# One Strassen product for the v of all attention heads, in place of four plain ones, and a new order of scores and transposes

## The chip, the cores and the metric

The kernel runs on one core of one Trainium2 chip, as one launch. The metric is the device time of the launch in microseconds (us). TensorE, VectorE, ScalarE and GpSimd are named PE, DVE, ACT and POOL in the profile's rows; PEld is TensorE's load of a stationary operand, SP the queue that issues most DMAs.

## The reference

A trunk of two layers on x of 512 tokens by 1024 features, in float32. Each layer is a SwiGLU FFN (hidden width 2816), a mixer, and a second FFN; after each of the six steps stands a layer norm over `alpha * x + step`. The mixer of layer 0 is block-sparse attention with a relative-position bias, that of layer 1 a pooling mixer. With 512 tokens in blocks of 256 the block selection always takes the one past block, so the attention is plain causal attention:

```
qkv = (h @ w_in).reshape(B, S, 3, H, dh)      # w_in 1024 x 3072, H = 8 heads of dh = 128
p   = softmax(q @ k.T * dh**-0.5 + bias[head, distance]), causal
out = concat_heads(p @ v) @ w_out
```

So v of all heads together is one product of h (512 x 1024) with 1024 columns of w_in.

## The kernel before

**Arithmetic.** Every float32 product is made of three matmuls on a high and a low part (`mm3`, lines 105 to 107: high with low, high with high, low with high). `split` (lines 100 and 101) forms the parts: ACT copies the high part, DVE subtracts it from the source for the low one. A weight tile of 128 x 1024 (512 KB) is loaded raw by SP, split into a pair, and called a unit. The FFNs already use Strassen's algorithm in Winograd's form, seven products for eight: a class `Seven` keeps an activation as the operands of the seven products, some of them sums made by `sums` on DVE (`form`, line 314), and a `Quad` holds the weights of one such product in five raw tiles, two of them summed as they are loaded by a GpSimd DMA with accumulation (line 208), and two more sums made on DVE (line 143). A `Plain` activation has only its high and low parts.

**Attention** (`attention`, from line 711) takes the heads in four pairs. For a pair it forms q and k of both heads, feature major (`a_block`: 24 matmuls with 512 tokens moving; in the first pair the tokens come in two halves of 256, since the layer norm before is still being finished), then v of the pair, token major (`values`, line 721: 96 matmuls in two groups of 48, the stationary operand 128 tokens of x, 256 weight columns moving). `scores(h)` is 12 matmuls and a softmax on DVE and ACT (lines 752 to 756). `transposes(h)` turns the probabilities through TensorE (10 transposes, line 764) and splits them; `outputs(h)` is 12 matmuls with v. The order in a pair is: scores of head h, first half of v, scores of head h+1, second half of v, transposes of h; transposes of h+1 and the outputs of both stand among the q and k of the next pair. After the four pairs comes the product with w_out (`BProduct`: `early` for the first four of its eight weight rows, 24 matmuls for each of four token tiles, and `tail`).

**What sets the order.** TensorE's order is that of the program. The instructions of DVE, ACT, POOL and the DMA queues are ordered by the compiler's list scheduler, each engine's queue then runs in order; `tc.issue_after` keeps the instructions of a block behind a given one on its engine. Weight units are split ahead of their use by `run_ahead`, up to `PARTS` = 5 beyond those that were given back by `retire`; raw tiles are loaded ahead by `load_ahead`, at most 9 not yet used up while no slots are held, 6 while `held[0]` is 4, as it is in attention. All of it shares 20 slots of 4 KB per partition. A second pool, `act`, of 9 tiles of 8 KB holds activations; two split weight units stand there as guests (named w) when attention begins. The layer norm's result is staged in `stage` (one tile of 16 KB).

**PSUM.** The eight banks are assigned by hand: in pairs 1 to 3, q and k in 0 and 1, v in 0 and 1, scores in 2, 3 and 4 (4, 5 and 6 for head 0), transposes in 5, 6 and 7, outputs in 2 and 3.

Of the kernel before, what the change touches and what calls it, by code (L numbers as in the profile page):

```python
# [32 lines left out]
P = 128  # L33
S = 512
D = 1024
# [48 lines left out]
def trunk(ctx, tc, x_in, xt, rel_bias, ln_g, ln_b, w_gu, w_dq, w_down, a_in, a_out, b_in, b_group, b_scale, b_out, onehot, out):  # L84
# [80 lines left out]

    def ffn_units(l, m):
# [3 lines left out]
        for i, jj in ORDER:  # L170
# [4 lines left out]
            else:  # L175
                if i == 1:
                    both = [Quad(w_dq[l, m, 2 * (jj - FF) + q]) for q in range(2)]
                    pieces[-10:] = [q.pieces[k] for k in range(5) for q in both]
# [5 lines left out]
    for hp in range(H // 2):  # L184
        for part in (0, 1, 2):
            a_plain(a_in[0], part * D + hp * 256)
    b_plain(a_out[0], range(NK))
# [49 lines left out]
    def run_ahead():  # L237
        load_ahead()
        while len(parts) < min(len(units), retired[0] + PARTS + max(0, free() - 2) // 2 + early[0] + sum(i >= retired[0] for i in guests)):
            prepare()  # L240
            load_ahead()
# [29 lines left out]
    class Plain:  # L271
# [14 lines left out]
        def put(self, t, half, src):  # L286
            hi, lo = self.parts_of(half)
            split(hi[:, :, t * P:(t + 1) * P], lo[:, :, t * P:(t + 1) * P], src)
# [5 lines left out]
    class Seven(Plain):  # L294
# [30 lines left out]
        def seven(self, b11, b21, b12, b22, room):  # L325
# [18 lines left out]
            yield  # L344

# [84 lines left out]
    def halves(x, accs, blocks):  # L430

        for i in range(8):
            a_block(x, accs[i % 4], *blocks[i % 4], 0, 256, range(4 * (i // 4), 4 * (i // 4) + 4))
            if i in LATE:
                late.pop(0)()
                if i == LATE[1]:
                    run_ahead()
# [17 lines left out]
    class BProduct:  # L455
# [35 lines left out]
        def tail(self):  # L491
# [5 lines left out]
            run_ahead()  # L497
# [213 lines left out]
    def attention(n, x, dest):  # L711
        held[0] = 4
        with tc.tile_pool(name="att", bufs=1) as ap:
# [7 lines left out]
            def values(hp, vp, tt):  # L721
                acc = bank(tt, f"v{hp}_{tt}")
                for i in range(2):
                    t = 2 * tt + i
                    for k in range(NK):
                        hi, lo = vp[k // 4]
                        c = slice((k % 4) * 256, (k % 4) * 256 + 256)
                        mm3(acc[:, i * 256:(i + 1) * 256], *x.at(k, t * P, (t + 1) * P), hi[:, c], lo[:, c], k == 0, k == NK - 1)
                if tt == 0:
                    v[hp] = [ap.tile([P, NT, 256], F32R, tag=f"v{i}", name=f"v{i}_{hp}") for i in range(2)]  # L730
                split(v[hp][0][:, 2 * tt:2 * tt + 2, :], v[hp][1][:, 2 * tt:2 * tt + 2, :],
                      acc.rearrange("p (t c) -> p t c", c=256))

            def scores(h):
# [4 lines left out]
                b0 = 2 if h else 4  # L739
# [36 lines left out]
            def outputs(h, b):  # L776
                o = bank(b, f"o{h}")
                vh, vl = v[h // 2]
# [211 lines left out]
```

## Time and profile before

| | |
|---|---|
| time, median of 3 runs | 1702.57 us (1699.46 to 1703.05) |
| profiled execution, its time | 1703.53 us |
| its span, first to last instruction | 1701.8 us |
| TensorE matmuls busy | 1681.0 us (99%) |
| TensorE weight loads busy | 1563.6 us (92%) |
| VectorE busy | 1328.7 us (78%) |
| ScalarE busy | 854.1 us (50%) |
| GpSimd busy | 125.8 us (7%) |
| DMA, mean | 164 GB/s |

A matmul's own duration in the trace is longer than the distance to the next one, since matmuls are pipelined: what one costs is read from the distance between starts, that is, from the length of a stretch with a known count. Attention's pairs stand from 346 to 519 us in the span, its product with w_out behind them.

### The profile page before, as it was taken

How to read it: one execution, taken by the hardware profiler on the slowest of the kernel's cores; microseconds unless marked ns; L12 is line 12 of the kernel's file. 1: busy time of each engine (PE TensorE's matmuls, PEld its weight loads, DVE VectorE, ACT ScalarE, POOL GpSimd, SP SyncE). 2: the span in 40 equal slices, each digit the busy share in tenths (PEclk: the TensorE clock that was granted, in tenths of full speed). 3: DMA queues.
4: the chain of work that ended last, by engine and by line, in shares of the span. 5: the costliest groups of instructions: out<-in, count | busy, mean ns of one | idle time of the engine just before them, and what ended most of it. 6: DMA issues, size and time to landing. Idle time of an engine off the chain costs nothing. (4 is left out here: it accounts for less than half of the span.)

```text
span 1701.8 us, 28140 instructions
## 1 busy us (share of the span) xinstructions
PE 1681.0 (99%) x11451; PEld 1563.6 (92%) x11451; DVE 1328.7 (78%) x1756; ACT 854.1 (50%) x1187; POOL 125.8 (7%) x168
## 2 busy tenths in 40 slices
PE   9999999999999999999999999999999999999997
PEld 9999899898888999989989999799898899998986
DVE  7686988775666878788788787897887887879696
ACT  5454555463444555545555555455454555545460
POOL 1102000000000001100000011000000101111000
PEclk9999999999999999999999999999999999999999
DMA  9779756512345267786683677756624647867541
GB/s 311 190 209 254 199 143 179 178 57 72 109 119 179 51 181 201 191 216 153 160 235 76 176 199 190 214 151 151 221 75 111 174 124 182 215 161 210 150 136 74
DMA packets 91058, 279.87 MB, mean 164 GB/s; under 512 B 8816, under 2 KB 26264, under 8 KB 90928
## 3 DMA queue, kind: packets, MB, share of 16 engines
q1 hardware_dynamic: 71088, 206.07, 36.2%
q0 software_dynamic: 19840, 71.99, 23.6%
q8 instruction: 90, 1.47, 0.4%
q14 instruction: 40, 0.33, 0.1%
HBM read 275.91 MB, written 4.74 MB: 165 GB/s over the span
## 5 line engine op out<-in xcount | busy, mean ns | idle before, releaser
L100 ACT ACTIVATE hi<-raw 128x1024 fp32r<-128x1024 f32 (+1 forms) x469 | 490.0, 1054 | 417.6 <-DVE lo L101 139.6
L101 DVE TENSOR_TENSOR lo<-raw,hi 128x1024 fp32r<-128x1024 f32 (+1 forms) x469 | 568.1, 1218 | 147.8 <-ACT hi L100 138.2
L105 PE MATMUL gu<-x,hi 128*128 128x256 f32 x2344 | 664.1, 283 | 1.2 <-DVE cb L570 0.8
L107 PE MATMUL gu<-x,lo 128*128 128x256 f32 x2344 | 663.6, 283 | 0.8 <-DVE lo L101 0.8
L106 PE MATMUL gu<-x,hi 128*128 128x256 f32 x2344 | 663.4, 283 | 0.0
L105 PEld LDWEIGHTS gu<-x,hi 128*128 128x128 f32 x2344 | 450.0, 192 | 3.7 <-DVE cb L570 1.7
L107 PEld LDWEIGHTS gu<-x,lo 128*128 128x128 f32 x2344 | 449.9, 192 | 1.4 <-DVE lo L101 1.4
L106 PEld LDWEIGHTS gu<-x,hi 128*128 128x128 f32 x2344 | 450.1, 192 | 0.4
L107 PE MATMUL d<-hi,xh 128*128 128x512 f32 x448 | 175.1, 391 | 7.4 <-DVE xh L101 7.4
L105 PE MATMUL d<-lo,xh 128*128 128x512 f32 x448 | 174.8, 390 | 0.2
L106 PE MATMUL d<-hi,xh 128*128 128x512 f32 x448 | 174.5, 389 | 0.0
L143 DVE TENSOR_TENSOR raw<-raw,raw 128x1024 f32<-128x1024 f32 x112 | 136.9, 1222 | 36.9 <-DMA raw<-in_ffn_w_dq 35.0
L208 POOL DMA_DIRECT2D raw<-in_ffn_w_gu x80 | 69.4, 868 | 801.1 <-DMA raw<-in_ffn_w_gu 404.5
L107 PEld LDWEIGHTS d<-hi,xh 128*128 128x128 f32 x448 | 84.1, 188 | 27.4 <-DVE xh L101 10.0
L105 PEld LDWEIGHTS d<-lo,xh 128*128 128x128 f32 x448 | 84.1, 188 | 17.9 <-DVE ca L570 0.6
L106 PEld LDWEIGHTS d<-hi,xh 128*128 128x128 f32 x448 | 84.1, 188 | 17.1
L567 ACT ACTIVATE kept<-gu 128x512 f32<-128x512 f32 x120 | 70.4, 586 | 48.7 <-PE gu L107 48.7
L105 PE MATMUL acc<-lo,h 128*128 128x512 f32 x192 | 75.2, 392 | 0.0
L107 PE MATMUL acc<-hi,h 128*128 128x512 f32 x192 | 74.7, 389 | 0.0
L106 PE MATMUL acc<-hi,h 128*128 128x512 f32 x192 | 74.7, 389 | 0.0
L642 DVE SCALAR_TENSOR_TENSOR ax<-d,ax 128x512 f32<-128x512 f32 x112 | 72.5, 683 | 0.0
L101 DVE TENSOR_TENSOR x<-st,x 128x512 fp32r<-128x512 f32 (+1 forms) x61 | 51.3, 854 | 20.2 <-ACT x L100 19.8
(169 smaller groups left out, 2301.5 us busy)
## 6 DMA issues: line engine op xcount, KB each, us to landing
raw<-in_ffn_w_gu SPq DMA_DIRECT2D x215, 512.0 KB, 4.9
raw<-in_ffn_w_gu POOLq DMA_DIRECT2D x80, 512.0 KB, 6.9
raw<-in_ffn_w_dq SPq DMA_DIRECT2D x80, 512.0 KB, 4.3
raw<-in_ffn_w_dq POOLq DMA_DIRECT2D x32, 512.0 KB, 8.3
raw<-in_ffn_w_down SPq DMA_DIRECT2D x24, 512.0 KB, 4.2
raw<-in_a_w_in SPq DMA_DIRECT2D x24, 512.0 KB, 4.7
ax<-in_ln_b POOLq DMA_DIRECT2D x20, 512.0 KB, 8.1
raw<-in_a_w_out SPq DMA_DIRECT2D x8, 512.0 KB, 5.3
```

The source lines that it names most:

```text
L100: nc.scalar.activation(hi, src, AF.Copy)
L101: return nc.vector.tensor_tensor(lo, src, hi.bitcast(F32), op=ALU.subtract)
L105: nc.tensor.matmul(acc, sh, ml, start=first, stop=False, skip_group_check=shared)
L106: nc.tensor.matmul(acc, sh, mh, start=False, stop=False, skip_group_check=shared)
L107: nc.tensor.matmul(acc, sl, mh, start=False, stop=last, skip_group_check=shared)
L143: nc.vector.tensor_tensor(d, d, more, op=ALU.add)
L208: queued["acc"] = nc.gpsimd.dma_start(p.tile, p.plus, accum_op=ALU.add)
L567: nc.scalar.activation(kept[i, jj], acc, AF.Copy)
L642: nc.vector.scalar_tensor_tensor(r, acc[t], 0.5 / ALPHA * sign, r, op0=ALU.mult, op1=ALU.add)
```

## The change

v of all eight heads is formed at once behind q and k of the first pair, by seven Strassen products. Each has two weight units (halves of the contraction), 24 matmuls with 128 tokens stationary and 512 weight columns moving, and accumulates in two banks. The attention's input becomes `Mixed`: the plain parts, which serve q and k and three of the products, and four summed operands. The weights come from a new input that holds the v columns of w_in rearranged into two quads. Partial results are kept in SBUF (`keep`) and added to later ones on DVE (`added`); `value` splits the sums into v. Scores of heads 0 and 1 and the transposes of head 0 stand between the seven products. In pairs 1 to 3 the order is: q and k of head h; outputs of h-2, transposes of h-1, scores of h; q and k of h+1; outputs of h-1, transposes of h, scores of h+1. Behind the last pair the token tiles of the product with w_out come in the order 0, 1, 3, 2, with the outputs of head 6 and the transposes of head 7 after the first. In `halves`, which the pooling mixer uses too, the weight units beyond the next two and the sums are placed behind the last split of the input. Signature and input lists are left out here, and so are empty lines.

```diff
@@ -162,6 +162,11 @@
     ORDER += [(i, FF + g) for g in range(1, BLOCK // GROUP) for i in LATER]
+    def two_quads(w, i):
+        both = [Quad(w[i + q]) for q in range(2)]
+        pieces[-10:] = [q.pieces[k] for k in range(5) for q in both]
+        return both
@@ -174,16 +179,20 @@
                 if i == 1:
-                    both = [Quad(w_dq[l, m, 2 * (jj - FF) + q]) for q in range(2)]
-                    pieces[-10:] = [q.pieces[k] for k in range(5) for q in both]
+                    both = two_quads(w_dq[l, m], 2 * (jj - FF))
                 for q in both:
                     q.unit(i)
         b_plain(w_down[l, m], range(BLOCK, NF))
     ffn_units(0, 0)
     for hp in range(H // 2):
-        for part in (0, 1, 2):
+        for part in (0, 1):
             a_plain(a_in[0], part * D + hp * 256)
+        if hp == 0:
+            both = two_quads(w_v, 0)
+            for i in LATER:
+                for q in both:
+                    q.unit(i)
     b_plain(a_out[0], range(NK))
@@ -234,9 +243,9 @@
-    def run_ahead():
+    def run_ahead(most=99):
         load_ahead()
-        while len(parts) < min(len(units), retired[0] + PARTS + max(0, free() - 2) // 2 + early[0] + sum(i >= retired[0] for i in guests)):
+        while len(parts) < min(len(units), taken[0] + most, retired[0] + PARTS + max(0, free() - 2) // 2 + early[0] + sum(i >= retired[0] for i in guests)):
             prepare()
@@ -285,7 +294,7 @@
             hi, lo = self.parts_of(half)
-            split(hi[:, :, t * P:(t + 1) * P], lo[:, :, t * P:(t + 1) * P], src)
+            self.last = split(hi[:, :, t * P:(t + 1) * P], lo[:, :, t * P:(t + 1) * P], src)
@@ -343,6 +352,18 @@
+    class Mixed(Seven):
+        put = Plain.put
+        def stationary(self, i, k, t):
+            if i in (4, 5, 6, 7):
+                o = self.parts[i][:, :, k, t * P:(t + 1) * P]
+                return o[:, 0], o[:, 1]
+            half, h = {1: (0, 0), 2: (1, 0), 3: (1, 1)}[i]
+            return self.at(4 * half + k, (2 * h + t) * P, (2 * h + t + 1) * P)
     def to_feature_major(dest, t, half, xn, n):
@@ -427,14 +448,18 @@
-    def halves(x, accs, blocks):
+    def halves(x, accs, blocks, sums=lambda: None):
         for i in range(8):
             a_block(x, accs[i % 4], *blocks[i % 4], 0, 256, range(4 * (i // 4), 4 * (i // 4) + 4))
             if i in LATE:
                 late.pop(0)()
                 if i == LATE[1]:
-                    run_ahead()
+                    while len(parts) < taken[0] + 2:
+                        prepare()
+                    with tc.issue_after(x.last.ins):
+                        run_ahead()
+                        sums()
         for acc, blk in zip(accs, blocks):
@@ -494,7 +519,7 @@
             early[0] = self.guests
-            run_ahead()
+            run_ahead(6)
             for t in range(NT):
@@ -718,25 +743,61 @@
-            def values(hp, vp, tt):
-                acc = bank(tt, f"v{hp}_{tt}")
-                for i in range(2):
-                    t = 2 * tt + i
-                    for k in range(NK):
-                        hi, lo = vp[k // 4]
-                        c = slice((k % 4) * 256, (k % 4) * 256 + 256)
-                        mm3(acc[:, i * 256:(i + 1) * 256], *x.at(k, t * P, (t + 1) * P), hi[:, c], lo[:, c], k == 0, k == NK - 1)
-                if tt == 0:
-                    v[hp] = [ap.tile([P, NT, 256], F32R, tag=f"v{i}", name=f"v{i}_{hp}") for i in range(2)]
-                split(v[hp][0][:, 2 * tt:2 * tt + 2, :], v[hp][1][:, 2 * tt:2 * tt + 2, :],
-                      acc.rearrange("p (t c) -> p t c", c=256))
+            accs, kept = {}, {}
+            def keep(i, acc):
+                kept[i] = ap.tile([P, 2, 512], F32, tag=f"kept{i % 5}", name=f"vkept{i}")
+                for t in range(2):
+                    nc.scalar.activation(kept[i][:, t], acc[t], AF.Copy)
+            def value(t, d, src, sign):
+                hi, lo = v["hi"][:, t, d * 512:(d + 1) * 512], v["lo", t // 2][:, t % 2, d * 512:(d + 1) * 512]
+                if sign == 1:
+                    split(hi, lo, src)
+                else:
+                    nc.scalar.activation(hi, src, AF.Copy, scale=-1.0)
+                    nc.vector.scalar_tensor_tensor(lo, src, -1.0, hi.bitcast(F32), op0=ALU.mult, op1=ALU.subtract)
+            def added(i, acc):
+                k = kept.pop(i)
+                for t in range(2):
+                    nc.vector.tensor_tensor(k[:, t], k[:, t], acc[t], op=ALU.add)
+                return [k[:, t] for t in range(2)]
+            def v_product(i):
+                if i in (1, 2, 5):
+                    accs[BANKS[i]] = [bank({1: 0, 2: 2, 5: 2}[i] + t, f"v{i}_{t}") for t in range(2)]
+                acc = accs[BANKS[i]]
+                for q in range(2):
+                    wh, wl = weights()
+                    for k in range(2):
+                        c = slice(k * 512, (k + 1) * 512)
+                        for t in range(2):
+                            mm3(acc[t], *x.stationary(i, 2 * q + k, t), wh[:, c], wl[:, c], q == 0 and k == 0 and i in (1, 2, 5),
+                                q == 1 and k == 1 and i in (2, 3, 4), True)
+                if i == 2:
+                    v["hi"] = lnp.tile([P, NT, D], F32R, tag="stage", name="vh")
+                if i in (2, 7):
+                    v["lo", len(v) - 1] = glob.tile([P, 2, D], F32R, tag="act", bufs=ACT, name=f"vl{len(v) - 1}")
+                if i in (1, 6, 5):
+                    keep(i, acc)
+                else:
+                    srcs = acc if i == 4 else added({2: 1, 7: 5, 3: 6}[i], acc)
+                    t0, d, sign = {2: (0, 0, 1), 7: (2, 1, -1), 3: (2, 0, 1), 4: (0, 1, -1)}[i]
+                    for t in range(2):
+                        value(t0 + t, d, srcs[t], sign)
+                with tc.issue_after(x.last.ins):
+                    retire(2)
             def scores(h):
                 (qh, ql), (kh, kl) = qk["q", h], qk["k", h]
                 bt = ap.tile([P, S], F32, tag="bias", bufs=2, name=f"bias{h}")
                 nc.sync.dma_start(bt, bass.AP(tensor=gr.tensor, offset=gr.offset + h * P * GW + P - 1,
                                                 ap=[[GW - 1, P], [1, S]]))
-                b0 = 2 if h else 4
+                b0 = 2 if h > 1 else 4
                 b01 = bank(b0, f"s{h}_01")
@@ -775,10 +836,9 @@
                 o = bank(b, f"o{h}")
-                vh, vl = v[h // 2]
-                vc = slice((h % 2) * P, (h % 2 + 1) * P)
+                vc = slice(h * P, (h + 1) * P)
                 for j, (m0, two) in enumerate(pT[h]):
-                    mm3(o[:, m0:], vh[:, j, vc], vl[:, j, vc], two[0], two[1], j == 0, j == NT - 1)
+                    mm3(o[:, m0:], v["hi"][:, j, vc], v["lo", j // 2][:, j % 2, vc], two[0], two[1], j == 0, j == NT - 1)
                 if h % 2 == 0:
@@ -792,37 +852,41 @@
                 if hp == 0:
-                    accs = [bank(i, f"qk0_{i}") for i in range(4)]
-                    for acc, nm in zip(halves(x, accs, blocks), names):
+                    qk_accs = [bank(i, f"qk0_{i}") for i in range(4)]
+                    for acc, nm in zip(halves(x, qk_accs, blocks, x.sums), names):
                         project(acc, *nm)
+                    with tc.issue_after(x.last.ins):
+                        retire(4)
+                    scores(0)
+                    for i in LATER:
+                        v_product(i)
+                        if i == 2:
+                            scores(1)
+                        if i == 7:
+                            transposes(0)
                 else:
                     for i in range(4):
+                        acc = bank(i + 2 if hp == 1 and i < 2 else i % 2, f"qk{hp}_{i}")
+                        a_block(x, acc, *blocks[i])
+                        project(acc, *names[i])
                         if i == 1:
-                            transposes(h - 1)
-                        if i == 2:
-                            outputs(h - 2, 2)
-                        if i == 3:
-                            ins = outputs(h - 1, 3)
+                            ins = outputs(h - 2, 4 if hp == 1 else 0)
                             if hp > 1:
                                 update_residual(ins, 2)
-                        acc = bank(i % 2, f"qk{hp}_{i}")
-                        a_block(x, acc, *blocks[i])
-                        project(acc, *names[i])
-                retire(4)
-                vp = [weights(), weights()]
-                scores(h)
-                values(hp, vp, 0)
-                scores(h + 1)
-                values(hp, vp, 1)
-                retire(2)
-                transposes(h)
+                            transposes(h - 1)
+                            scores(h)
+                        if i == 3:
+                            retire(4)
+                            outputs(h - 1, 0)
+                            transposes(h)
+                            scores(h + 1)
             held[0] = 0
             out_p = BProduct(n, NK, lambda f: (oT[f // 2][:, 0, f % 2, :], oT[f // 2][:, 1, f % 2, :]), 1.0, dest, 3)
             pre = [out_p.take(f) for f in range(NK - R)]
-            for t in (1, 0, 3, 2):
-                if t == 0:
+            for t in (0, 1, 3, 2):
+                if t == 1:
+                    outputs(H - 2, 4)
                     transposes(H - 1)
-                    outputs(H - 2, 4)
                 if t == 3:
@@ -912,7 +976,7 @@
-    xs = [cls(f"{i}") for i, cls in enumerate((Seven, Plain, Seven, Seven, Plain, Seven))] + [None]
+    xs = [cls(f"{i}") for i, cls in enumerate((Seven, Mixed, Seven, Seven, Plain, Seven))] + [None]
@@ -968,6 +1032,12 @@
     return x.reshape(2, 256, 2, 4, P).transpose(2, 0, 4, 3, 1).reshape(4, P, 1024)
+def v_quads(w):
+    w = w[0, :, 2 * D:].reshape(2, 2, 2, P, 2, 512)
+    return w.transpose(1, 4, 0, 3, 2, 5).reshape(2, 4, P, 1024)
@@ -975,7 +1045,7 @@
     inputs = dict(inputs, onehot=bucket_onehot(), xt=blocks(np.asarray(inputs["x"])[0]), ffn_w_gu=quads(np.asarray(inputs["ffn_w_gu"])),
-                  ffn_w_dq=down_quads(np.asarray(inputs["ffn_w_down"])))
+                  a_w_v=v_quads(np.asarray(inputs["a_w_in"])), ffn_w_dq=down_quads(np.asarray(inputs["ffn_w_down"])))
     nc = bacc.Bacc("TRN2", target_bir_lowering=False, num_devices=1, dynamic_dma_scratch_size=4096)
```

## Rows read from the trace of the kernel before

**Rows 1.** The page's head: span, and the engines' busy time.
```profile
span 1701.8 us, 28140 instructions
PE 1681.0 (99%) x11451; PEld 1563.6 (92%) x11451; DVE 1328.7 (78%) x1756; ACT 854.1 (50%) x1187; POOL 125.8 (7%) x168
```

**Rows 2.** Waits of TensorE in the whole span: total us, times, longest us.
```profile
PE d L107 <- DVE xh L101: 7.4, 6, 1.6
PE s L105 <- DVE pr L752: 0.7, 3, 0.2
...
PEld s L105 <- DVE pr L752: 1.6, 3, 0.6
```

**Rows 3.** Busy time by stretch, all engines; the stretches are runs of one work each.
```profile
core 0: us, PE busy (x) PEld busy (x) DVE busy (x) ACT busy (x) POOL busy (x), PEclk, DMA share, GB/s
373.16:378.90 5.74, 5.74 (x49) 5.74 (x48) 5.74 (x13) 5.19 (x10) 0.00 (x0) 1.00 0.64 189
409.03:414.48 5.45, 5.45 (x27) 4.50 (x26) 0.69 (x1) 0.60 (x1) 0.39 (x2) 1.00 0.23 69
378.90:380.84 1.94, 1.94 (x14) 1.81 (x13) 1.94 (x6) 0.80 (x3) 0.00 (x0) 1.00 0.19 68
399.70:401.64 1.94, 1.94 (x14) 1.81 (x12) 1.05 (x2) 1.59 (x4) 0.01 (x1) 1.00 0.00 0
386.59:387.60 1.01, 1.01 (x13) 1.01 (x11) 0.82 (x4) 0.65 (x2) 0.00 (x0) 1.00 0.88 301
371.21:518.82 147.61, 146.96 (x912) 132.60 (x911) 93.33 (x202) 66.75 (x137) 5.91 (x16) 1.00 0.37 106
```

**Rows 4.** Timeline of TensorE: the scores of head 7, first, waiting, and the following instruction.
```profile
509.62 0.28 PE L105 MATMUL s<-k,q 128*128 128x256 f32 x1
...
511.26 0.50 PE L105 MATMUL s<-k,q 128*128 128x512 f32 x1 [0.24 <-DVE pr L752]
...
512.05 0.28 PE L105 MATMUL v<-lo,x 128*128 128x256 f32 x1
```

**Rows 5.** Groups by line and shape: busy us, mean ns of one (v: attention's stretch alone).
```profile
L101 DVE TENSOR_TENSOR lo<-raw,hi 128x1024 fp32r<-128x1024 f32 x467 | 566.8, 1220 | 145.3 <-ACT hi L100 135.7 <-PE gu L107 4.8 <-PE gu L106 2.9
L143 DVE TENSOR_TENSOR raw<-raw,raw 128x1024 f32<-128x1024 f32 x112 | 136.9, 1222 | 36.9 <-DMA raw<-in_ffn_w_dq 35.0
L570 DVE TENSOR_TENSOR ca<-gu,kept 128x512 f32<-128x512 f32 x80 | 55.0, 687 | 7.8 <-PE gu L107 7.6
L314 DVE SCALAR_TENSOR_TENSOR st<-st 128x1024 f32<-128x1024 f32 x16 | 19.6, 1224 | 0.4
...
L101 DVE TENSOR_TENSOR v<-v,v 128x512 fp32r<-128x512 f32 x8 | 5.5, 682 | 0.2 <-ACT v L100 0.2
```

**Rows 6.** Busy time by stretch as above: three stretches that matter for VectorE.
```profile
359.20:414.40 55.20, 55.20 (x362) 50.86 (x361) 25.76 (x57) 19.77 (x41) 0.82 (x4) 1.00 0.21 64
275.00:315.00 40.00, 40.00 (x179) 33.10 (x178) 39.79 (x43) 25.46 (x27) 1.21 (x3) 1.00 0.73 222
582.80:593.60 10.80, 10.80 (x92) 10.80 (x92) 10.25 (x11) 6.50 (x7) 0.00 (x0) 1.00 0.16 50
```

**Rows 7.** Timeline of VectorE around the end of the first pair's q and k.
```profile
363.40 0.69 DVE L101 TENSOR_TENSOR q<-qk,q 128x512 fp32r<-128x512 f32 x1 [3.32 <-ACT q L100]
366.29 0.69 DVE L101 TENSOR_TENSOR k<-qk,k 128x512 fp32r<-128x512 f32 x1 [2.19 <-ACT k L100]
...
373.18 2.35 DVE L101 TENSOR_TENSOR lo<-raw,hi 128x1024 fp32r<-128x1024 f32 x2
...
388.18 1.79 DVE L101 TENSOR_TENSOR p<-pt,p 128x512 fp32r<-128x512 f32 x4
```

**Rows 8.** The weights of attention: guests' last use; DMAs from 300 to 346 us; accumulating loads.
```profile
L107 PE MATMUL qk<-x,w x32: 279/283/283, 348.1 to 369.7; 128*128 128x256 f32 x32
...
raw<-in_a_w_in SPq DMA_DIRECT2D x12, 512.0 KB, 5.2
...
raw<-in_ffn_w_dq POOLq DMA_DIRECT2D x32, 512.0 KB, 8.3
```

**Rows 9.** Timeline of VectorE: last normalisation of head 7's probabilities.
```profile
521.10 0.48 DVE L756 TENSOR_SCALAR pr<-pr,sm 128x512 f32<-128x512 f32 x1
```

More of the change, by code (lines that the diff above doesn't have):

```diff
@@ L83, in trunk @@
 @with_exitstack
-def trunk(ctx, tc, x_in, xt, rel_bias, ln_g, ln_b, w_gu, w_dq, w_down, a_in, a_out, b_in, b_group, b_scale, b_out, onehot, out):
+def trunk(ctx, tc, x_in, xt, rel_bias, ln_g, ln_b, w_gu, w_dq, w_down, w_v, a_in, a_out, b_in, b_group, b_scale, b_out, onehot, out):
     nc = tc.nc
@@ L946, in trunk @@
         phase(i, xs[i], xs[i + 1])
-_INS = ["x", "xt", "rel_bias", "ln_g", "ln_b", "ffn_w_gu", "ffn_w_dq", "ffn_w_down", "a_w_in", "a_w_out",
+_INS = ["x", "xt", "rel_bias", "ln_g", "ln_b", "ffn_w_gu", "ffn_w_dq", "ffn_w_down", "a_w_v", "a_w_in", "a_w_out",
         "b_w_in", "b_w_group", "b_scale", "b_w_out", "onehot"]
```

## Prediction

> **What bounds the kernel now.** I began with the page's head: of a span of 1701.8 us matmuls are busy 99%, in 11451 instructions, while DVE has 78% and ACT less [rows 1]. Next the waits of TensorE over the whole span: the longest kind totals 7.4 us and is in the FFNs, and in attention there is one kind only, scores that wait for the softmax before them to leave their banks [rows 2]. So TensorE's stream is the bound almost everywhere, and a change is worth what it takes out of that stream, less what it makes TensorE wait. Then the stretches of one work each, for the price of each piece of the stream: 48 v matmuls with 256 columns take 5.74 us, 0.1196 us each; 24 q or k matmuls with 512 columns take 5.45 us, 0.2271 us each; a head's scores take 1.94 us, its outputs 1.94, its transposes 1.01 [rows 3]. From the start of head 0's scores to the first matmul of the product with w_out, 147.61 us pass [rows 3]. The reader is to see that 512 columns cost less than twice what 256 do: 0.2392 less 0.2271, so 0.0121 us is saved whenever two short matmuls become a long one, apart from Strassen's eighth.
>
> **The change part by part. The v product on TensorE.** Before: 4 pairs of 96 matmuls, 384 x 0.1196 = 45.92 us. After: 7 products of 2 units x 2 slices x 2 token tiles x 3 = 24 matmuls, 168 x 0.2271 = 38.15 us. That is -7.77 us. Of it, 5.74 are the product left out and 2.0 the longer matmuls (168 x 0.0121).
>
> A rule of the Trainium skill (TensorE: Matmul & The Clock Gate, section Back-to-back issue gap) puts the isolated distance at columns over 2.4 GHz plus about 2.5 ns, 109.2 and 215.8 ns here; by it this term would be 41.9 less 36.3, an estimate of -5.7 us. The rows have a larger fixed part, about 13 ns in either form, and the sum goes by them.
>
> **Scores, transposes and outputs** keep their counts, and q and k theirs. What goes is a wait. In pairs 1 to 3 the scores of head h+1 come 5.74 us after those of head h and use the same banks: head 7's take from 509.62 to 512.05, 2.43 us in place of 1.94, and wait for DVE's reading of head 6's scores [rows 4]. The wait is there 3 times [rows 2]: 3 x 0.49 = -1.47 us. After the change two blocks of q and k, 10.9 us, lie between. Head 1's scores stand 10.9 us behind head 0's too. Late next would be k of the same head: in a pair the scores follow its split with outputs and transposes between, 1.94 + 1.01 = 2.95 us of cover; a split of q is one ACT and one 0.69 us DVE instruction [rows 7]. Nothing charged; between 0 and 1.1 us in pair 1, where bank 4 goes from the outputs of head 0 to the scores of head 2 (the upper end: four splits of probabilities, 1.79 us, ahead of the outputs' split [rows 7], less the 0.7 us that the cover leaves). The outputs' bank 0 has the same cover or more.
>
> **What DVE gets.** Between 359.2 and 414.4 us it is busy 25.76 of 55.2 us [rows 6]. By the steps above the second pair will begin at its end: 371.21 + 2 x 1.94 + 7 x 5.45 + 1.01 = 414.3. Added there: 4 sums and 4 splits of the input, 8 x 1.22 = 9.8; two weight sums for each of two quads, 4 x 1.22 = 4.9; six adds of kept products, 6 x 0.69 = 4.1; eight splits of v at 0.68, 5.5; and ten more weight splits than now, 12.2 (14 units for v are to be split, and the next pair's first, where four are split now) [rows 5]. That is 36.5 us. Moved out behind 414: two splits of v (1.4), head 1's probabilities (1.8), two outputs (1.4), three q and k (2.1), 6.7 in all [rows 5, 7]. The sum is 55.6 us of durations, in a stretch of 55.2. But neighbours overlap: two splits of 1.22 take 2.35 [rows 7], so the 22 long ones that are added cost 0.09 each less, 2.0, and the 14 short ones, by the same overlap, 1.2: about 52.4 of 55.2, 95%. DVE sits idle now where the input sums fit: 3.32 us before the split of q, 2.19 before each of the next [rows 7]. The same eight instructions at the head of the next FFN take 10.8 us [rows 6], so here from 360 to 371; they are first needed by the third product, 15 us later. The last of them needs a tile that a guest unit leaves, which is used until 369.7 at the latest [rows 8].
>
> **Does TensorE wait for that?** The nearest stretch is in the FFN's down product, with the same seven products of 24 matmuls and two units each: from 275 to 315 us DVE is busy 39.79 of 40 us, and TensorE starts some 176 matmuls, 0.227 us each, without one wait [rows 6]. That says the cost can be nothing. On the other side, a softmax is in the way here twice, and the units beyond three ahead are split just in time: for each product two units, 2.3 us of DVE in 5.45. If the two units of the third product come behind head 0's softmax, or those of the fifth behind head 1's, I get a delay of up to 4 us. ACT is no bound: 19.77 us of 55.2 now [rows 6]. I take +1.0 us, nearer the down product's row, with 0 and 4 as bounds.
>
> **The weights' way.** 12 tiles of w_in are loaded between 300 and 346 us, by SP's queue, each 5.2 us to landing [rows 8]; the limit of 9 still holds there. In the new order these are the first pair's four and the first eight of the ten v tiles, so the four accumulating loads (8.3 us to landing in the FFN [rows 8]) are issued ahead of the first product too. POOL has 0.82 us of work in the stretch [rows 6]. Cost nothing; the cover is some 30 us, and without it the first rival below comes about. 3.1 MB more are moved (14 loads of 0.5 MB for 8), where the DMA share is 0.21 [rows 6].
>
> **The end of attention.** Head 7's scores are now followed by 24 matmuls and head 6's outputs, 5.45 + 1.94 = 7.39 us, and then its transposes, of which the last four need the last row of probabilities, 0.6 us later. Now that row is ready at 521.58, 9.5 us after head 7's scores end [rows 4, 9]. Some of what DVE does in between (v, head 6's softmax) falls away, and four weight splits come ahead of it. So 1.5 us late by the row as it is, 0 if DVE is freer, 2.5 if all four weight splits stand before it. I take +1.0 us.
>
> **The pooling mixer** has its unit splits reordered at the start of its layer: nothing there waits on TensorE now [rows 2], so 0, within 0.3.
>
> **Sum.** -7.77 - 1.47 + 1.0 + 1.0 = -7.24 us. The profiled execution's own time is 1703.53 us, 1.73 above its span and 0.96 above the median of the runs: 1696.3 by the execution, 1695.3 by the median. I say 1696.
>
> **Rivals.** (a) Weights late, slower than before. If the summed weight tiles are loaded not ahead but under the limit of 6, as units are given back, their chain is exposed: load 5.2, accumulate 8.3, two sums 2.3, split 2.4, 18.2 us. Begun at 374, when the first product gives slots back, it ends at 392, 6 us after the third product's turn at 386. The tiles of the fifth product are then loaded when the third's units have been split, and 5.2 + 8.3 + 2.4 = 16 us stand against two products, 10.9: 5 us more. With the forecast's other 2 us, 1703.5 - 9.2 + 13 = 1707.3. It decides if the first accumulating load for v is issued after about 368 us (18.2 ahead of 386) in place of before 346. Against it: 12 loads by 346 [rows 8].
>
> (b) DVE becomes the bound of the first pair: its 95% is then more than it can do with its waits for ACT, and TensorE follows it through the third to sixth product. Price: 10% of the stretch, 5.5 us in place of 1, 1700.8. For it: the sum of durations is over the stretch's length. Against it: the 40 us at 99% without a wait [rows 6]. A page of the Trainium skill (Perfetto Trace Analysis, section Identifying the Most-Contended Engine) says to take as bound the engine with the highest occupancy, judging TensorE by its weight loads; by that rule this rival is what happens. The trace does not bear it out as it stands: DVE has 39.79 us to the weight loads' 33.10 in that stretch, and the matmuls keep their distance.
>
> (c) All is hidden: neither the first pair nor head 7 costs anything. 1703.5 - 9.2 = 1694.3.
>
> **How the numbers follow.** Forecast (1694.8 to 1699) 0.62; (c) 0.13; (b) 0.18; (a) 0.07. The range for eight in ten, 1692 to 1701: below it only a gain that none of the parts has, above it (a) and the worst part of (b). About 0.2% (3.4 us) is what a measurement of this kernel tells from no change. The forecast and (c) are faster; of (b) a third (losses under 5 us) is faster, the rest the same; (a) is slower: faster 0.81, same 0.12, slower 0.07.
>
> **What would show it.** The profile after should have 11235 matmuls, and 168 of v with 512 columns in 38.2 us; the wait of scores for the softmax should be gone; head 0's scores to the first matmul with w_out should take about 139 to 141 us in place of 147.61; DVE should be above nine tenths from 359 to 414 us, with TensorE's waits there on DVE's weight splits under 4 us; head 7's transposes should wait about 1 us for the last normalisation. The prediction is wrong if v matmuls with 512 columns start more than 0.23 us apart, if TensorE waits for a weight DMA, or if the stretch behind attention gets longer.

## The result and the profile after

The changed kernel takes 1693.74 us, median of 4 runs (1692.04 to 1694.34), the kernel before beside it 1702.73 us, median of 4 (1699.46 to 1703.05): a ratio of 0.995, with a 95% interval of 0.9933 to 0.9967, or 5.6 to 11.4 us gained. 1696 was forecast, with 1692 to 1701 as range. The profiled execution took 1694.32 us.

The head of the page of the changed kernel, to be held against [rows 1]:

```profile
span 1692.5 us, 27752 instructions
...
PE 1671.5 (99%) x11235; PEld 1547.8 (91%) x11235; DVE 1353.7 (80%) x1780; ACT 865.8 (51%) x1203; POOL 129.6 (8%) x172
```

216 matmuls fewer (384 short ones have become 168 long ones), and TensorE still fills 99% of the span. Its waits in the whole span (total us, times, longest), as in [rows 2]:

```profile
PE d L107 <- DVE xh L101: 7.1, 7, 1.6
...
PE o L105 <- DVE pr L813: 0.5, 1, 0.5
PE pt L825 <- DVE pr L817: 0.3, 1, 0.3
```

The scores' wait for the softmax has gone. Two rows of attention are new, and both belong to its end: head 6's outputs (o) and head 7's transposes (pt).

Busy time by stretch of the changed kernel: the first pair; from head 0's scores to the first matmul with w_out; the product with w_out up to its last matmul's start; and all that follows.

```profile
core 0: us, PE busy (x) PEld busy (x) DVE busy (x) ACT busy (x) POOL busy (x), PEclk, DMA share, GB/s
359.20:414.40 55.20, 55.20 (x305) 48.30 (x304) 53.89 (x83) 36.64 (x59) 0.00 (x0) 1.00 0.41 126
371.40:509.50 138.10, 138.10 (x695) 117.97 (x695) 105.05 (x206) 72.73 (x144) 5.93 (x16) 1.00 0.43 122
509.50:560.90 51.40, 50.64 (x243) 42.14 (x243) 36.03 (x72) 25.23 (x51) 3.90 (x6) 1.00 0.57 154
560.90:1692.50 1131.60, 1115.30 (x7698) 1041.70 (x7696) 915.59 (x1159) 570.58 (x756) 83.34 (x96) 1.00 0.62 164
```

The same view of the kernel before, the two stretches that [rows 3] don't have:

```profile
518.82:569.00 50.18, 50.18 (x244) 42.27 (x243) 31.22 (x58) 23.44 (x45) 3.86 (x6) 1.00 0.55 151
569.00:1701.80 1132.80, 1115.70 (x7698) 1041.70 (x7696) 915.27 (x1159) 570.61 (x756) 83.20 (x96) 1.00 0.61 164
```

The ends of these windows are rounded. In the changed kernel's timeline head 0's scores and the first and the last matmul with w_out start at

```profile
371.36 0.28 PE L105 MATMUL s<-k,q 128*128 128x256 f32 x1
509.54 0.39 PE L105 MATMUL acc<-lo,oT 128*128 128x512 f32 x1
560.88 0.39 PE L107 MATMUL acc<-hi,oT 128*128 128x512 f32 x1
```

and in the kernel before at 371.21, 518.82 and 569.03. So the two spans differ by +0.15 us ahead of the scores, -9.43 in the scores, v and projections (147.61 to 138.18), +1.13 in the product with w_out (50.21 to 51.34) and -1.15 in all that follows: -9.30. The last figure isn't the change's: the same work there took between 1129.5 us (the run plain512) and 1133.4 us (dve_plus6) in the other kernels below. What the change did is -9.43 + 1.13 = -8.3 us.

Look at the first row: in the first pair VectorE is busy 53.89 of 55.20 us, 98% (25.76 before [rows 6]), and TensorE all of it. The stretch from the scores on has no wait at all: 138.10 us of matmuls in 138.10.

The v matmuls of the changed kernel (a third of them; duration in ns, first and last start):

```profile
L105 PE MATMUL v<-lo,x x56: 387/389/477, 373.3 to 413.8; 128*128 128x512 f32 x56
```

Three such groups make the 168. From 373.3 to the end of the last triple at 414.5 is 41.2 us, less head 1's scores and head 0's transposes (1.94 + 1.01 [rows 3]) 38.25 us, where 38.15 was forecast.

The end of attention, timeline of TensorE in the changed kernel:

```profile
514.76 0.39 PE L107 MATMUL acc<-hi,oT 128*128 128x512 f32 x1
515.63 0.51 PE L105 MATMUL o<-p,vh 128*128 128x512 f32 x1 [0.49 <-DVE pr L813]
515.97 0.40 PE L106 MATMUL o<-p,vh 128*128 128x512 f32 x1
...
517.68 0.82 PE L825 MATMUL pt<-ident,pr 128*128 128x128 f32 x6
518.77 0.66 PE L825 MATMUL pt<-ident,pr 128*128 128x128 f32 x4 [0.28 <-DVE pr L817]
519.18 0.48 PE L105 MATMUL acc<-lo,oT 128*128 128x512 f32 x1
```

A wait costs more than its row says. The outputs begin 0.87 us after the matmul ahead of them, where 0.23 is the distance, and their second follows 0.34 later in place of 0.23: 0.64 + 0.11 = 0.75 us for a wait shown as 0.49. The ten transposes take 1.50 us in place of 1.01. Together 1.24, where the whole product with w_out got 1.13 longer. And VectorE in that time:

```profile
506.39 2.36 DVE L101 TENSOR_TENSOR lo<-raw,hi 128x1024 fp32r<-128x1024 f32 x2 [0.26 <-ACT hi L100]
...
509.87 2.35 DVE L101 TENSOR_TENSOR lo<-raw,hi 128x1024 fp32r<-128x1024 f32 x2
512.14 1.27 DVE L101 TENSOR_TENSOR p<-pt,p 128x384 fp32r<-128x384 f32 x3
513.32 0.61 DVE L813 SCALAR_TENSOR_TENSOR pr<-s,bias 128x128 f32<-128x128 f32 x2
...
518.23 0.49 DVE L817 TENSOR_SCALAR pr<-pr,sm 128x512 f32<-128x512 f32 x1
```

Head 7's scores are done at 509.5, but four weight splits and head 6's probabilities stand ahead of its softmax, which begins at 513.32. It reads bank 4, and head 6's outputs want that bank; its last normalisation ends at 518.7, and the last four transposes want that.

### The profile page after: what moved, and what is told of

The parts are those of the page before. It is cut to its first block, busy times and chain, and to the rows that moved or that the text cites. A ratio compares the mean times of both kernels' runs of the same rounds, so it can differ in the third digit from the quotient of the medians.

```text
span 1692.5 us, 27752 instructions
## 1 busy us (share of the span) xinstructions
PE 1671.5 (99%) x11235; PEld 1547.8 (91%) x11235; DVE 1353.7 (80%) x1780; ACT 865.8 (51%) x1203; POOL 129.6 (8%) x172
## 5 line engine op out<-in xcount | busy, mean ns | idle before, releaser
L100 ACT ACTIVATE hi<-raw 128x1024 fp32r<-128x1024 f32 (+1 forms) x475 | 496.5, 1054 | 415.5 <-DVE lo L101 142.1
L101 DVE TENSOR_TENSOR lo<-raw,hi 128x1024 fp32r<-128x1024 f32 (+1 forms) x475 | 575.4, 1219 | 147.7 <-ACT hi L100 137.4
L143 DVE TENSOR_TENSOR raw<-raw,raw 128x1024 f32<-128x1024 f32 x116 | 141.8, 1222 | 37.0 <-DMA raw<-in_ffn_w_dq 35.1
L101 DVE TENSOR_TENSOR x<-st,x 128x512 fp32r<-128x512 f32 (+1 forms) x65 | 56.0, 877 | 22.8 <-ACT x L100 22.5
```

The costliest lines, as they stand in the source:

```text
L100: nc.scalar.activation(hi, src, AF.Copy)
L101: return nc.vector.tensor_tensor(lo, src, hi.bitcast(F32), op=ALU.subtract)
L143: nc.vector.tensor_tensor(d, d, more, op=ALU.add)
```

## The experiments

Each kernel has one edit. "The stretch" is from the start of head 0's scores to that of the first matmul with w_out, 147.61 us before and 138.18 after; the windows shown have rounded ends. Its noise is small: in the seven variants of the changed kernel below in which TensorE doesn't wait there, it took 138.10 to 138.19 us. A time is a median, and its ratio, with a 95% interval, is to the kernel before measured beside it, whose medians lay between 1700.9 and 1703.0 us.

**1. Strassen's eighth alone.** In the changed kernel v is formed by eight plain products, 192 matmuls with 512 columns; the input sums fall away, and head 1's scores and head 0's transposes take new places among the products.

```
-            both = two_quads(w_v, 0)
-            for i in LATER:
-                for q in both:
-                    q.unit(i)
+            for d in range(2):
+                for kh in range(2):
+                    for q in range(2):
+                        plain(w_v[q, 2 * d + kh])
...
                     scores(0)
+                    v_plain(0)
+                    scores(1)
+                    v_plain(1)
```

> v of all heads at once with 512 columns moving, but as eight plain products (192 matmuls) in place of seven Strassen ones: no sums of the input, no summed weights, no kept products. If the change's gain is TensorE's own count, the stretch from head 0's scores to the first matmul with w_out is one product, 24 x 0.2271 = 5.45 us, longer than in the changed kernel (138.1 us): about 143.6, against 147.61 before; the time is 1.2 to 4.5 us under the kernel before. Rival: VectorE's added work already costs the changed kernel something that no wait shows; then this one loses clearly less than 5 us against it, about 140 to 141.5 us in the stretch.

1698.35 us (ratio 0.998, 0.997 to 0.9989). The stretch by its busy time:

```profile
370.90:514.50 143.60, 143.60 (x720) 122.55 (x719) 89.88 (x188) 64.04 (x132) 5.92 (x16) 1.00 0.38 107
```

143.60 - 138.18 = 5.4 us for 24 matmuls, 0.226 each: the eighth gives what TensorE's count says, and the sums and splits that it needs give nothing of it back in this stretch. Without it 147.61 - 143.60 = 4.0 us are left: the scores' wait and the longer matmuls.

**2. The scores' banks alone.** The kernel before, with the scores of heads 2, 4 and 6 in banks 5 to 7.

```
-                b0 = 2 if h else 4
+                b0 = 2 if h % 2 else 5 if h else 4
```

> The kernel before, with the scores of heads 2, 4 and 6 in banks 5 to 7 in place of 2 to 4, so that the next head's scores share no bank with them. If the wait of scores for the softmax is a term of its own, the stretch of 147.61 us becomes 146.1 (three times 0.49 us less) and no row of TensorE's waits names scores; the time falls by 1.5 us, within what a measurement can tell from no change. Rival: the wait only moves to the transposes or outputs behind it, which use the same banks; the stretch stays at 147 or more.

1701.84 us (ratio 0.9999, 0.9989 to 1.0008): the time can't show it. The stretch can, and has no wait left:

```profile
371.10:517.20 146.10, 146.10 (x912) 132.69 (x911) 92.76 (x201) 66.77 (x137) 5.93 (x16) 1.00 0.37 107
```

From start to start (371.07 to 517.21) it is 146.14 us, 1.47 less than before, the term of 1.47. With run 1 that leaves 4.0 - 1.5 = 2.5 us for the longer matmuls, which no run has alone; 192 x 0.0121 is 2.3.

**3. The input sums late.** The four sums and four splits of the input, which the changed kernel makes between 361.3 and 371.7 us, are put behind the split of the first pair's last k.

```
-                    for acc, nm in zip(halves(x, qk_accs, blocks, x.sums), names):
-                        project(acc, *nm)
+                    for acc, nm in zip(halves(x, qk_accs, blocks), names):
+                        lo = project(acc, *nm)
+                    with tc.issue_after(lo.ins):
+                        x.sums()
```

> The changed kernel with the four input sums and their splits placed behind the split of the first pair's last k, at about 372 us, in place of 361. If it is VectorE's idle time between 360 and 371 us that makes the sums free, about 9 us of its work now falls into a stretch that is 97% full: TensorE waits at the third product and the ones behind it, 5 to 9 us in all. Rival: VectorE catches up, since softmax and later splits give way; under 2 us.

1699.53 us (ratio 0.9987, 0.9978 to 0.9997). Its stretch, and TensorE's waits there:

```profile
371.10:515.00 143.90, 139.62 (x697) 117.83 (x696) 112.82 (x212) 76.44 (x148) 5.91 (x16) 1.00 0.41 118
```
```profile
PE v L105 <- DVE lo L101: 3.4, 2, 2.6
PE s L105 <- DVE pr L814: 0.9, 2, 0.5
```

The stretch is 5.7 us longer than in the changed kernel, the time 5.8: two thirds of the gain are gone. So the sums cost nothing because they stand between 360 and 371 us, where VectorE had been idle. Eight instructions at the distance of 1.13 us that neighbours keep (two take 2.35 [rows 7]) are 9.0 us; 5.7 came through. The other 3.3 us were taken up by slack, the time by which VectorE's work is done ahead of the matmul that needs it.

**4. More work for VectorE.** Two or six dummy adds of 128x1024 in the changed kernel, first with no place of their own (dve_plus), then behind the split of the last k (dve_behind_k); one execution of each.

```
+                    dummy = ap.tile([P, 2, 512], F32, tag="kept0", name="dummy")
+                    nc.gpsimd.memset(dummy, 0.0)
+                    with tc.issue_after(lo.ins):
+                        for _ in range(6):
+                            nc.vector.tensor_tensor(dummy, dummy, dummy, op=ALU.add)
```

> The changed kernel with two extra additions of 128 x 1024 on VectorE (some 2.3 us) behind the second product; their result is not used. In the changed kernel VectorE is 97 to 98% busy from 359 to 414 us and the first unit of the fifth product is split only about half a us before its turn. If that is the slack, TensorE waits 1 to 2 us more, and the stretch from head 0's scores to the product with w_out is 139.5 to 140 us. Rival: splits run ahead far enough, nothing changes (138.1).

> As the run with two extra additions, but six of them, some 6.8 us. If VectorE has about half a us of slack, TensorE waits 5.5 to 6.5 us more: a stretch of about 144 us. Rival: softmax and later splits give way, TensorE waits under 3 us, a stretch of 141 or less.

1692.27 and 1695.16 us, the stretch 138.2 in both. They tell nothing: without a dependency the adds were issued at 319 us, before attention.

> Two extra additions of 128 x 1024 on VectorE, 2.3 us, held behind the split of the first pair's last k, so at about 373 us (in the earlier runs they had run in an idle stretch at 319 us). Moving 9.1 us of sums to this place cost 5.8 us, so VectorE has some 3.3 us of slack here: TensorE waits 0 to 0.5 us more, the stretch from head 0's scores to the product with w_out stays at 138.1 to 138.6. Rival, since VectorE is 98% busy here: every added microsecond is paid, 140.4.

> Six extra additions at the same place, 6.8 us. With 3.3 us of slack TensorE waits 3 to 4 us more: a stretch of 141 to 142 us. If every microsecond is paid 144.9; if VectorE gives way elsewhere under 139.

1694.32 and 1695.97 us. Two adds, at 377.0 us, change nothing: 138.2. Six, from 377.6 to 385.8 us, make the stretch 141.8 and bring waits back, of head 1's scores (s) for banks that head 0's softmax still reads, and of the third product (v) for the split of its second weight unit:

```profile
PE s L105 <- DVE pr L814: 1.6, 2, 1.1
PE v L105 <- DVE lo L101: 0.8, 1, 0.8
```

Six adds are 6.8 us in the same way; 3.6 came through, so the slack is 3.2 us, the 3.3 of run 3 by another way. VectorE at 98% is not the bound of the first pair, but only 3 us away from being it. What waits first and longest here is not a product for its weights, as in the prediction's step, but head 1's scores, 1.6 of 2.4 us.

**5. The weights late.** The summed weights of v are held back by a gate in `load_ahead`. In late_weights it opens at the first `retire(4)`; in weights_behind_k also a small DMA that reads the split of k stands ahead on SP's queue.

```
-        while len(loaded) < len(pieces) and ...
+        while len(loaded) < (gate[0] or len(pieces)) and ...
...
-                    with tc.issue_after(x.last.ins):
+                    gate[0] = 0
+                    mark = dram.tile([1, 64], F32, name="mark")
+                    behind = nc.sync.dma_start(mark, qk["k", 1][1][0:1, 0:64].bitcast(F32))
+                    with tc.issue_after(x.last.ins), tc.issue_after(behind.ins):
                         retire(4)
```

> The changed kernel, but the summed weight tiles of v (and what comes after them) are not loaded before the first pair's q and k give their units back, at about 371 us, so the accumulating loads come after that. By the rival's price in the prediction TensorE waits 6 us at the third and 5 us at the fifth product: 9 to 13 us in all, and the time returns to that of the kernel before or above it. Against it: if the splits that are ahead hide most of the chain, under 4 us.

1692.68 us (ratio 0.9946, 0.9931 to 0.9961), the stretch 138.2 without a wait. The gate moved the first pair of summed tiles little (accumulated at 350.7 and 352.1 us; in the changed kernel all four go between 323.7 and 328.8, the line below), the second to 381.6 and 382.9, and even that was early enough for the fifth product.

```profile
L217 POOL DMA_DIRECT2D raw<-in_a_w_v x4: 866/866/866, 323.7 to 328.8; - x4
```

> The changed kernel with the summed tiles of v loaded only behind a small DMA that reads the first pair's last k, so at about 373 us in fact (in the run with late weights they still started at 346, since the queue was free and only the program's order had been changed). The chain load 5, accumulate 8 to 9, two sums 2.3, split 2.4 then ends at about 391, 5 us after the third product's turn; the fifth product's tiles follow the third's splits: 4 to 5 us more. By the rival's price in the prediction 9 to 13 us are lost. Rival: the second chain is hidden, because the second set of tiles is loaded before the third product is split; then 4 to 6 us.

1699.23 us (ratio 0.999, 0.9981 to 0.9999), the stretch 145.4, 7.2 longer. The accumulating loads are issued from 375.9 us on, and VectorE waits for them:

```profile
385.02 2.48 DVE L143 TENSOR_TENSOR raw<-raw,raw 128x1024 f32<-128x1024 f32 x2 [7.81 <-DMA raw<-in_a_w_v]
387.43 1.22 DVE L101 TENSOR_TENSOR lo<-raw,hi 128x1024 fp32r<-128x1024 f32 x1
```

TensorE around its one wait, the third product, and then its granted clock (the column after POOL's):

```profile
384.14 0.40 PE L107 MATMUL s<-k,q 128*128 128x512 f32 x1
388.70 0.80 PE L105 MATMUL v<-lo,x 128*128 128x512 f32 x1 [4.16 <-DVE lo L101]
389.29 0.63 PE L106 MATMUL v<-hi,x 128*128 128x512 f32 x1
389.71 0.63 PE L107 MATMUL v<-hi,x 128*128 128x512 f32 x1
390.14 0.63 PE L105 MATMUL v<-lo,x 128*128 128x512 f32 x1
...
394.96 0.40 PE L105 MATMUL v<-lo,x 128*128 128x512 f32 x1
```
```profile
388.70:390.00 1.30, 1.30 (x3) 1.12 (x4) 1.30 (x2) 0.13 (x1) 0.00 (x0) 0.50 1.10 217
390.00:392.00 2.00, 2.00 (x6) 1.54 (x6) 2.00 (x3) 2.00 (x3) 0.00 (x0) 0.50 1.03 240
...
394.00:396.00 2.00, 2.00 (x9) 1.65 (x8) 2.00 (x3) 1.58 (x2) 0.00 (x0) 0.85 0.31 108
396.00:400.00 4.00, 4.00 (x20) 3.29 (x19) 4.00 (x11) 2.90 (x7) 0.00 (x0) 1.00 0.00 0
```

The third product begins 4.56 us after the matmul ahead of it, 4.33 more than the distance of 0.23. The engine then runs at half its clock, 1.2 GHz, matmuls 0.43 us apart, until about 394.5: fifteen of them take 6.26 us (388.70 to 394.96) in place of 15 x 0.2271 = 3.41, 2.85 more. 4.33 + 2.85 = 7.2, all of it. The fifth product doesn't wait.

**6. The end of attention.** In the last pair the four units are given back behind head 7's scores (retire_late), or two ahead and two behind (retire_split), so that fewer weight splits stand ahead of the softmax; or head 7's scores stand ahead of head 6's transposes (scores_first, one execution).

```
                         if i == 3:
-                            retire(4)
+                            if hp < 3:
+                                retire(4)
...
                             scores(h + 1)
+                            if hp == 3:
+                                retire(4)
```

> The changed kernel with one line moved: in the last pair the weight units are given back behind the scores of head 7 and not ahead of the outputs of head 5, so that four weight splits no longer stand ahead of head 7's softmax on VectorE. In the changed kernel TensorE waits 0.5 us at the outputs of head 6 and 0.3 us at the transposes of head 7. If the splits cause it, both waits go and the stretch behind attention is 0.9 us shorter; the time falls by as much, too little to be told. Rival: the splits are then late for the product with w_out, and TensorE waits there, up to 2 us.

1694.17 us (ratio 0.9957, 0.994 to 0.9974). Both waits of the end are gone, and a longer one has come, for the weight splits that were put off; from the first to the last matmul with w_out it takes 52.7 us (508.1 to 560.8), 51.3 in the changed kernel:

```profile
PE acc L105 <- DVE lo L101: 2.4, 1, 2.4
```

> The changed kernel with two of the last pair's four weight units given back ahead of the outputs of head 5 and two behind the scores of head 7. Moving all four removed the 0.8 us of waits for head 7's softmax and brought 2.4 us of waiting for weights. If two splits ahead are enough for both, neither wait is left and the stretch from the first matmul with w_out to the next FFN is 0.9 us shorter than in the changed kernel; the time can't show it. Rival: part of each wait stays, and nothing is gained.

1695.09 us (ratio 0.9966, 0.9952 to 0.998), the same wait with 2.3 us, and 54.3 us (508.7 to 563.0): the clock fell behind this one, to a mean of 0.64 over the next 4.7 us, between its levels of 1.00 (2.4 GHz) and 0.50 (1.2 GHz). In retire_late it stayed at 1.00. First retire_split, then retire_late:

```profile
515.28:520.00 4.72, 4.72 (x16) 4.06 (x17) 1.97 (x4) 0.28 (x2) 0.00 (x0) 0.64 0.37 116
514.70:520.00 5.30, 5.30 (x32) 4.77 (x33) 2.79 (x6) 1.98 (x5) 0.41 (x2) 1.00 0.33 101
```

In the third kernel the scores move:

```
                             outputs(h - 1, 0)
+                            if hp == 3:
+                                scores(h + 1)
                             transposes(h)
-                            scores(h + 1)
+                            if hp < 3:
+                                scores(h + 1)
```

> The changed kernel, but in the last pair head 7's scores stand ahead of head 6's transposes, 1.01 us earlier. On VectorE that puts most of head 7's softmax ahead of one weight split and of the splits of head 6's probabilities. Theory (the 1.2 us lost at the end of attention are a matter of VectorE's order: the softmax stood last): the last normalisation of head 7 comes some 0.6 to 1 us earlier, the waits of head 6's outputs for bank 4 (0.5 us) and of head 7's transposes (0.3 us) go, and from the first to the last matmul of the product with w_out 50.2 to 50.7 us pass in place of 51.4. Rival (VectorE has too much to do by then, in whatever order): the last two splits of head 6's probabilities now stand behind the softmax, TensorE waits 0.7 us or more for them in head 6's outputs, and the stretch stays at 51.2 to 51.8 us. The kernel's time, 1694 us within 2, can't tell the two apart; the waits can.

1694.63 us. Here VectorE's last normalisation does come early enough, and the transposes don't wait; what it was put ahead of is now late, head 6's probabilities:

```profile
514.68 0.51 PE L105 MATMUL o<-p,vh 128*128 128x512 f32 x1 [1.11 <-DVE p L101]
517.08 1.25 PE L825 MATMUL pt<-ident,pr 128*128 128x128 f32 x10
```

51.9 us with w_out (507.9 to 559.8). In all three orders VectorE has four weight splits, a set of probabilities and a softmax to do in the same time, and whatever stands last is waited for. None of the three shortens the product with w_out (52.7, 54.3 and 51.9 us for 51.3); their times can't be told from the changed kernel's.

## Why the prediction was right, and where it was off

**v on TensorE, -7.77.** Right. The stretch lost 9.43 us; 1.47 of it is the scores' wait (run 2), which leaves 7.96. The eighth was put at 5.74 of short matmuls; in long ones it measures 5.4 (run 1), and 2.5 are left for the longer matmuls where 2.3 were worked out. That bears out the distances of [rows 3]. The Trainium skill (TensorE: Matmul & The Clock Gate, section Back-to-back issue gap) has a fixed part of about 2.5 ns in the distance of an isolated matmul; by it the 192 long matmuls of run 1 would have gained 0.5 us by their length, an estimate that the trace doesn't bear out.

**The scores' wait, -1.47.** Right, shown alone in run 2.

**The first pair, +1.0.** This is the step that was off: it cost nothing, its lower bound, and the stretch took 138.2 us in place of the 139 to 141 that it was to take. VectorE's load was underestimated by 1.5 us (53.89 us for 52.4 worked out) and still didn't bind. Its sum has two errors, which make up 0.9 of that: between 359.2 and 414.4 us the trace has 16 weight splits for 4 before, twelve more and not ten (2.3 us), and six splits of v for two before, four more and not the six that it comes to (-1.4 us). The step took as dangerous that units are split just in time behind two softmaxes; what it did not work out is the slack, 3.2 us by run 4 and 3.3 by run 3, and with that in hand neither softmax came through. The row that it might have followed to the end is the down product's 40 us at 99% without a wait [rows 6].

**The idle time ahead of 371 us** as the place of the input sums: right, and worth 5.8 us (run 3).

**The end, +1.0.** The size was right (1.13), but in part by luck: of the 1.24 us of waits, 0.49 are head 7's transposes, for which the 1.0 was meant, and 0.75 head 6's outputs, which wait for bank 4 while the softmax reads it. The prediction followed that softmax to its last row only, and not to the bank that it holds.

**Rival (a), weights late.** Not what happened: all four accumulating loads were issued by 328.8 us. Its price was wrong in parts that run 5 tells apart. The third product came 4.3 us late for the 6 worked out; the fifth not at all for 5, since all the gated tiles were asked for together; and 2.85 us were lost to the clock, which wasn't foreseen. 7.2 in place of 11.

**Rival (b), VectorE the bound.** It didn't happen: 53.89 us of work in 55.20, to the weight loads' 48.30, and no wait; two more instructions on VectorE changed nothing, and with six more TensorE followed by 3.6 us. The Trainium skill (Perfetto Trace Analysis, section Identifying the Most-Contended Engine) would name VectorE the bound of this stretch; the trace doesn't agree.

**Rival (c), all hidden,** is nearest in time and half right: the first pair costs nothing, the end does. That its 1694.3 is the time of the profiled execution, 1694.32, is chance: the end's +1.13 and the -1.15 of work that the change doesn't touch all but cancel. The forecast's own range, 1694.8 to 1699, was missed by 1 us. Term by term the change did -7.96 for -7.77, -1.47 for -1.47, 0 for +1.0 and +1.13 for +1.0, so -8.3 for -7.24, and nearly all of the difference is the first pair's term. The remainder that the change doesn't touch moves by more than that between executions (1129.5 to 1133.4 us).

Left open: why the same work behind attention differs by up to 3.9 us between executions of neighbouring kernels. The traces show where: held against plain512 matmul by matmul, the changed kernel keeps the same distances there but at a few places in which TensorE waits in one and waits less, or not at all, in the other. One matmul waits 1.58 us for VectorE at 741.38 us, its twin in plain512 0.45 at 743.93; another waits 0.85 us at 730.58, its twin not at all.

## What to carry to other kernels

When TensorE's stream is full, count the stream: matmuls by their measured distance at each width, and the waits that go, gave the stretch's gain within 0.2 us (9.24 worked out, 9.43 measured) before anything else was weighed. For the engine that feeds it, ask not how busy it is but how far ahead of its consumer it stands: 98% with 3 us in hand cost nothing, and the hand was there because the new work could begin in idle time before the stretch. At a seam where softmax, splits and weights fall due together, ask what each of them holds: here three orders only changed which one was waited for.

## What was not expected of the hardware

- A single wait of TensorE of 4.16 us was followed by 5.8 us at a granted clock of 0.50 (1.2 GHz) while it had matmuls back to back, and cost 2.85 us beyond itself (run 5). The clock fell in retire_split too, after a wait of 2.34 us, though the first matmuls behind it, up to 516.3 us, still kept their 0.23 us: 0.64 on average from 515.28 to 520 us, some 1.7 us lost (4.72 x 0.36), which is why it ends later than retire_late. After waits of 2.61 us (run 3) and 2.36 us (retire_late) the matmuls that followed kept 1.00, so the length of the wait alone doesn't tell; what does stays open.
- A wait costs about 0.26 us more than the profile shows: the overlap with the matmul ahead is lost (0.39 us long, 0.23 to the next start) and the second matmul behind it is 0.11 us late (0.75 for 0.49 at head 6's outputs). By the distances between starts the three waits of run 4, shown as 1.13, 0.52 and 0.75 us, came to 1.39, 0.79 and 1.03; a fourth place, 0.17 us late without a wait in its row, to 0.28.
